# A hybrid encoder block: the first two token tiles normalised and transposed one by one, and the first loads in another order

## The chip, the cores and the metric

The kernel runs on one core of a Trainium2 chip. The metric is the device time of one execution in microseconds (us), lower is better; times shown are medians over runs. The engines are named as in the profile: PE is TensorE's matmul side and PEld its weight loads, DVE is VectorE, ACT is ScalarE, POOL is GpSimd, SP is SyncE, whose queue issues the loads of this part of the program.

## The reference, cut to what matters

One layer of a bidirectional encoder on 1024 tokens of width 1024, all in float32. Only its start is touched by the change: the first RMSNorm and the first columns of the combined input projection.

```python
def rmsnorm(x, g):
    xf = x.astype(jnp.float32)
    y = xf * lax.rsqrt(jnp.mean(xf * xf, axis=-1, keepdims=True) + EPS)
    return (y * g.astype(jnp.float32)).astype(x.dtype)
...
        h = rmsnorm(x, norm_mix[l])
        proj = h @ w_in[l]
        q, k, v, r, lr_f, lr_b, u, g_a, g_b = jnp.split(proj, split_points, axis=-1)
...
        o = (o * jax.nn.silu(r.astype(jnp.float32))).astype(x.dtype)
        y_a = o @ w_branch_gla[l]
...
        merged = jax.nn.sigmoid(g_a) * y_a + jax.nn.sigmoid(g_b) * y_b
        x = x + merged @ w_out[l]
        h2 = rmsnorm(x, norm_ffn[l])
        gate, up = jnp.split(h2 @ w_ffn_in[l], 2, axis=-1)
        x = x + (jax.nn.silu(gate) * up) @ w_ffn_out[l]
    return rmsnorm(x, norm_final)
```

Between the projection and `y_a` lies a gated linear attention in both directions with four heads, and beside it a pooling branch.

## The kernel before, in words

Every float32 product is made of three fp32r products: each operand is split into a high part (a cast on ACT) and a low part (the rest, a subtraction on DVE or POOL), and `mm3` (L293) issues high by high, high by low and low by high into one sum. Every instruction is written out by hand in the order in which its engine runs it; an engine works its list strictly in that order. Work that is to run beside matmuls stands in generators, which `pump` (L159), called after each `mm3`, advances by the columns that were multiplied; `begin` starts such a generator with a delay, `finish_side` runs the rest of it.

The 1024 tokens are eight tiles of 128, here called tile 0 to tile 7. Four buffers hold the raw tokens and four the normalised ones, so tile 4 uses the buffers of tile 0 (`x_126`, `xn_130` in the program's rows), tile 5 those of tile 1 (`x_127`, `xn_131`), 6 those of 2 (`x_128`, `xn_132`) and 7 those of 3 (`x_129`, `xn_133`). The first stage, which lasts to about 47 us, does this for every tile:

- **Norm** (`norm_x`, L393): ACT squares the tile with a row sum (L331), DVE adds the epsilon (`n1rs`, L322), POOL raises it to the power -0.5 (L323), DVE scales the tile (`xn`, L327). Then the load of the tile four further on is issued into the freed buffer. `norms` (L399) does two tiles as a generator.
- **Transposes** (`to_features`, L352, for a pair of tiles): for each of four pairs of feature blocks, four 128x128 transposes on PE (`transpose_tile`, L338) go into one PSUM bank, two for either tile. ACT then takes the bank out with the norm's gain as the high part `hh` (L345, two instructions of 128x256), DVE as the low part `hl` (L348, two of 128x256).
- **Values** (`first_values`, L415): eight feature blocks by three products, 24 matmuls of 288 columns (256 values of head 0 and 32 columns of the decay's low rank). The sum is split by ACT (`vh`, L198) and DVE (`vl`, L199), and ACT copies the low-rank columns (`lr`, L421); `lr` stands behind `vl` of the same tile.

The first weights come in four loads `raw` of 256 KB and one `lraw` of 128 KB with lines of 32 floats. Their high parts `fwh` are cast on ACT (L198, values) and POOL (L249, low rank), their low parts `fwl` made on DVE (the first two) and POOL (L199, L251).

Before the loop (L442 to L468) tiles 0 and 1 are normed and transposed together into four banks, and norms of 2 and 3 are written behind. In the loop over pairs (L469) the norms are two pairs ahead of their values: with tile 0 run the norms of 4 and 5, with tile 1 the transposes of 2 and 3, with tile 2 the norms of 6 and 7, with tile 3 the transposes of 4 and 5, with tile 5 those of 6 and 7. After tile 7 the projections of q and k of head 0 begin.

## Time and profile before

| what | value |
|---|---|
| median of 3 runs | 1399.84 us (1399.4 to 1400.83) |
| the profiled execution | 1400.29 us |
| its span, first to last instruction | 1398.6 us |
| PE busy | 1367.3 us, 98% of the span |
| PEld busy | 1152.5 us, 82% |
| DVE, ACT, POOL busy | 848.1, 624.0, 751.1 us |
| mean granted TensorE clock | 0.998 of full speed |

A row of the timeline gives the start, the time from start to end, engine, line, operation and operands of an instruction (or of a run of like ones, with xN), and in brackets how long the engine had been idle before it and what released it. Instructions of one engine overlap a little, so distances between starts say how fast it issues.

### The profile page before, as it was taken

How to read it: one execution, taken by the hardware profiler on the slowest of the kernel's cores; microseconds unless marked ns; L12 is line 12 of the kernel's file. 1: busy time of each engine (PE TensorE's matmuls, PEld its weight loads, DVE VectorE, ACT ScalarE, POOL GpSimd, SP SyncE). 2: the span in 40 equal slices, each digit the busy share in tenths (PEclk: the TensorE clock that was granted, in tenths of full speed). 3: DMA queues.
4: the chain of work that ended last, by engine and by line, in shares of the span. 5: the costliest groups of instructions: out<-in, count | busy, mean ns of one | idle time of the engine just before them, and what ended most of it. 6: DMA issues, size and time to landing. Idle time of an engine off the chain costs nothing. (4 is left out here: it accounts for less than half of the span.)

```text
span 1398.6 us, 18511 instructions
## 1 busy us (share of the span) xinstructions
PE 1367.3 (98%) x6654; PEld 1152.5 (82%) x6654; DVE 848.1 (61%) x1073; ACT 624.0 (45%) x1125; POOL 751.1 (54%) x565
## 2 busy tenths in 40 slices
PE   7999999999999999899999999999999999999997
PEld 6889898988888888788887888888888888888876
DVE  6266757667745885587875865556565556343364
ACT  6364655554334444455346633333333334453253
POOL 3261716041387555468665176666666667464364
PEclk9999999999999999999999999999999999999999
DMA  6211423322477668997425455554444447976461
GB/s 191 76 57 50 136 64 103 106 62 75 135 241 234 207 215 270 323 402 275 151 76 183 164 180 173 173 173 159 147 140 148 142 153 254 385 257 216 165 240 62
DMA packets 167453, 243.56 MB, mean 174 GB/s; under 512 B 10905, under 2 KB 97857, under 8 KB 167361
## 3 DMA queue, kind: packets, MB, share of 16 engines
q1 hardware_dynamic: 154944, 216.16, 46.3%
q10 hardware_dynamic: 12416, 26.22, 5.0%
q8 instruction: 52, 0.85, 0.3%
q14 instruction: 41, 0.33, 0.1%
HBM read 164.48 MB, written 77.86 MB: 173 GB/s over the span
## 5 line engine op out<-in xcount | busy, mean ns | idle before, releaser
L199 POOL TENSOR_TENSOR wl<-fs,wh 128x512 fp32r<-128x512 f32 x120 | 165.0, 1379 | 163.9 <-ACT wh L198 141.3
L291 PE MATMUL ps<-gl,wh 128*128 128x512 f32 x616 | 240.0, 390 | 0.8 <-DVE gl L1472 0.8
L291 PE MATMUL ps<-gh,wh 128*128 128x512 f32 x616 | 240.6, 391 | 0.0
L291 PE MATMUL ps<-gh,wl 128*128 128x512 f32 x616 | 239.9, 390 | 0.0
L199 POOL TENSOR_TENSOR wl<-fraw,wh 128x512 fp32r<-128x512 f32 x90 | 129.9, 1443 | 67.2 <-ACT wh L198 66.5
L199 POOL TENSOR_TENSOR ol<-gor,oh 128x1024 fp32r<-128x1024 f32 (+1 forms) x42 | 102.1, 2437 | 91.9 <-ACT oh L198 72.9
L291 PE MATMUL ps<-hh,wh 128*128 128x512 f32 x376 | 149.5, 398 | 0.0
L291 PE MATMUL ps<-hh,wl 128*128 128x512 f32 x376 | 146.8, 391 | 0.0
L291 PE MATMUL ps<-hl,wh 128*128 128x512 f32 x376 | 146.6, 390 | 0.0
L291 PEld LDWEIGHTS ps<-gl,wh 128*128 128x128 f32 x616 | 115.7, 188 | 24.9 <-DVE gl L1472 1.3
L291 PEld LDWEIGHTS ps<-gh,wl 128*128 128x128 f32 x616 | 115.7, 188 | 24.2
L199 POOL TENSOR_TENSOR wl<-raw,wh 128x512 fp32r<-128x512 f32 x44 | 61.4, 1411 | 137.7 <-ACT wh L198 135.2
L291 PEld LDWEIGHTS ps<-gh,wh 128*128 128x128 f32 x616 | 115.7, 188 | 23.6
L291 PE MATMUL ps<-oh,oh 128*128 128x512 f32 x308 | 120.0, 390 | 1.3 <-DVE x L1800 1.3
L291 PE MATMUL ps<-ol,oh 128*128 128x512 f32 x308 | 120.1, 390 | 0.2 <-DVE ol L199 0.2
L291 PE MATMUL ps<-oh,ol 128*128 128x512 f32 x308 | 119.9, 389 | 0.0
L199 POOL TENSOR_TENSOR wl<-wraw,wh 128x512 fp32r<-128x512 f32 x56 | 90.7, 1646 | 46.7 <-ACT wh L198 46.7
L199 DVE TENSOR_TENSOR ol<-wor,oh 128x1024 fp32r<-128x1024 f32 (+1 forms) x42 | 63.9, 1542 | 53.1 <-ACT oh L198 50.0
L198 ACT CAST wh<-fs 128x512 fp32r<-128x512 f32 x120 | 73.8, 615 | 30.8 <-DVE fs L902 23.1
L291 PEld LDWEIGHTS ps<-hh,wl 128*128 128x128 f32 x376 | 70.6, 188 | 15.1
L291 PEld LDWEIGHTS ps<-hl,wh 128*128 128x128 f32 x376 | 70.7, 188 | 13.4
L291 PEld LDWEIGHTS ps<-hh,wh 128*128 128x128 f32 x376 | 70.7, 188 | 13.4
(258 smaller groups left out, 3173.2 us busy)
## 6 DMA issues: line engine op xcount, KB each, us to landing
fraw<-in_w_ffn_in_dram SPq DMA_DIRECT2D x44, 512.0 KB, 6.4
gor<-g_out SPq DMA_DIRECT2D x35, 512.0 KB, 7.0
raw<-in_w_in_dram SPq DMA_DIRECT2D x48, 256.0 KB, 4.4
g_out<-s SPq DMA_DIRECT2D x44, 256.0 KB, 2.3
fraw<-in_w_in_dram SPq DMA_DIRECT2D x20, 512.0 KB, 4.2
wor<-t_out SPq DMA_DIRECT2D x20, 512.0 KB, 7.6
g_out<-g SPq DMA_DIRECT2D x33, 256.0 KB, 2.6
x<-in_x_dram SPq DMA_DIRECT2D x16, 512.0 KB, 3.9
```

What stands on the lines that cost most here:

```text
L198: nc.scalar.copy(hi, src)
L199: eng.tensor_tensor(lo, src, as_f32(hi), op=ALU.subtract)
L291: nc.tensor.matmul(ps, a[i], b[j], start=first and n == 0, stop=last and n == 2, skip_group_check=onto)
```

## The change

- **Loads.** The order on SP's queue is now tile 0, the norm's gain, the first two `raw`, `lraw`, the other two `raw`, and then tiles 1, 2 and 3. Tile 1 stood second before, and `lraw` behind all four `raw`.
- **Tiles 0 and 1 apart.** Each has its own two banks with four transposes each (`transpose_four`), and `hh` and `hl` of one feature block of one tile at a time, 128x128 (`gain_and_split_one`), eight of each per tile where eight of 128x256 served both. DVE's second low part of the weights stands between the second and third of these blocks of tile 0.
- **Squares apart from the norm.** `square_x` issues only ACT's part; `norm_x` does the rest.
- **Order of the rest.** Tile 1 is transposed behind the values of tile 0 on PE; the squares of 1, 2 and 3 stand behind tile 0's `hh` on ACT; DVE makes the norm of tile 3 between the fourth and fifth block of tile 1; the splits of the values of tile 0 stand behind all of this. The transposes of tiles 2 and 3 run beside the values of tile 1, from its fifth block on.
- **The loop** now starts at tile 2, and its norms are one pair ahead: those of 4 and 5 with tile 2, of 6 and 7 with tile 4. Their transposes run with tiles 3 and 5, as before.

From tile 2's first matmul on, PE's list is the same as before; ACT's differs up to the squares of 7, DVE's up to the norm of 7.

SP's queue at the start of the program; `x_126` to `x_129` are the loads of tiles 0 to 3. Before:

```order
L371 DMA x_126<-in_x_dram 128x1024
L374 DMA rows<-in_norm_mix_dram 8x128
L371 DMA x_127<-in_x_dram 128x1024
L206 DMA raw_141<-in_w_in_dram 128x2x256
L206 DMA raw_143<-in_w_in_dram 128x2x256
L206 DMA raw_145<-in_w_in_dram 128x2x256
L206 DMA raw_147<-in_w_in_dram 128x2x256
L384 DMA lraw_137<-in_w_in_dram 128x8x32
L371 DMA x_128<-in_x_dram 128x1024
L371 DMA x_129<-in_x_dram 128x1024
```

Now:

```order
L382 DMA x_126<-in_x_dram 128x1024
L388 DMA rows<-in_norm_mix_dram 8x128
L206 DMA raw_140<-in_w_in_dram 128x2x256
L206 DMA raw_142<-in_w_in_dram 128x2x256
L385 DMA lraw_137<-in_w_in_dram 128x8x32
L206 DMA raw_145<-in_w_in_dram 128x2x256
L206 DMA raw_147<-in_w_in_dram 128x2x256
L382 DMA x_127<-in_x_dram 128x1024
L382 DMA x_128<-in_x_dram 128x1024
L382 DMA x_129<-in_x_dram 128x1024
```

The load of tile 1 (`x_127`) moved from third place behind `lraw`, and `lraw` in front of the last two `raw`.

DVE behind the last `hl` of tile 0; `n1rs` and `xn` are the steps of a norm, `tr` a bank of transposes, `vl` the low part of a tile's values. Before (the `hl` of tiles 0 and 1 stand just ahead of this, all together):

```order
L322 TENSOR_SCALAR n1rs_254<-n1ms_252 128x1
L327 TENSOR_SCALAR xn_132<-x_128,n1rs_254 128x1024
L322 TENSOR_SCALAR n1rs_261<-n1ms_259 128x1
L327 TENSOR_SCALAR xn_133<-x_129,n1rs_261 128x1024
L322 TENSOR_SCALAR n1rs_275<-n1ms_273 128x1
L327 TENSOR_SCALAR xn_130<-x_126,n1rs_275 128x1024
L322 TENSOR_SCALAR n1rs_293<-n1ms_291 128x1
L327 TENSOR_SCALAR xn_131<-x_127,n1rs_293 128x1024
L199 TENSOR_TENSOR vl_162<-ps_266,vh_161 128x256
```

Now:

```order
L327 TENSOR_SCALAR n1rs_237<-n1ms_235 128x1
L332 TENSOR_SCALAR xn_131<-x_127,n1rs_237 128x1024
L327 TENSOR_SCALAR n1rs_269<-n1ms_242 128x1
L332 TENSOR_SCALAR xn_132<-x_128,n1rs_269 128x1024
L343 SCALAR_TENSOR_TENSOR hl_209<-tr_276,cols_173,hh_208 128x128 x2
L343 SCALAR_TENSOR_TENSOR hl_216<-tr_276,cols_173,hh_215 128x128 x2
L327 TENSOR_SCALAR n1rs_294<-n1ms_274 128x1
L332 TENSOR_SCALAR xn_133<-x_129,n1rs_294 128x1024
L343 SCALAR_TENSOR_TENSOR hl_222<-tr_277,cols_173,hh_221 128x128 x2
L343 SCALAR_TENSOR_TENSOR hl_228<-tr_277,cols_173,hh_227 128x128 x2
L199 TENSOR_TENSOR vl_162<-ps_244,vh_161 128x256
```

The norms of 4 and 5 (the third and fourth pair of rows before) are gone from here, those of 1 and 2 stand in their place, and the norm of 3 stands in the middle of tile 1's `hl`.

ACT from the squares of tiles 4 and 5 on (`xn_130,n1ms<-x_126` and `xn_131,n1ms<-x_127`); `vh` and `lr` are copies of a tile's finished values. Before, with the values of tiles 0 and 1 (`ps_266`, `ps_308`):

```order
L331 ACTIVATE xn_130,n1ms_273<-x_126 128x1024
L331 ACTIVATE xn_131,n1ms_291<-x_127 128x1024
L198 CAST vh_161<-ps_266 128x256
L421 COPY lr_158<-ps_266 128x128
L345 ACTIVATE hh_228<-tr_312,cols_173 128x256 x2
L345 ACTIVATE hh_234<-tr_327,cols_173 128x256 x2
L345 ACTIVATE hh_240<-tr_342,cols_173 128x256 x2
L345 ACTIVATE hh_246<-tr_357,cols_173 128x256 x2
L198 CAST vh_161<-ps_308 128x256
L421 COPY lr_158<-ps_308 128x128
L331 ACTIVATE xn_132,n1ms_389<-x_128 128x1024
L331 ACTIVATE xn_133,n1ms_407<-x_129 128x1024
```

Now, with the values of tiles 1, 2 and 3 (`ps_310`, `ps_386`, `ps_426`):

```order
L198 CAST vh_161<-ps_310 128x256
L446 COPY lr_158<-ps_310 128x128
L409 ACTIVATE xn_130,n1ms_390<-x_126 128x1024
L409 ACTIVATE xn_131,n1ms_408<-x_127 128x1024
L198 CAST vh_161<-ps_386 128x256
L446 COPY lr_158<-ps_386 128x128
L356 ACTIVATE hh_435<-tr_430,cols_173 128x256 x2
L356 ACTIVATE hh_452<-tr_447,cols_173 128x256 x2
L356 ACTIVATE hh_469<-tr_464,cols_173 128x256 x2
L356 ACTIVATE hh_486<-tr_481,cols_173 128x256 x2
L198 CAST vh_161<-ps_426 128x256
L446 COPY lr_158<-ps_426 128x128
```

The squares of 4 and 5 stood in front of `vh` of tile 0 and now stand behind `lr` of tile 1; those of 6 and 7 (`x_128`, `x_129`) moved from behind `lr` of tile 1 to behind `lr` of tile 3, just below the rows shown.

```diff
--- before.py
+++ after.py
@@ -198,7 +198,7 @@
         nc.scalar.copy(hi, src)
         eng.tensor_tensor(lo, src, as_f32(hi), op=ALU.subtract)
 
-    def load(src, kts, c0, width):
+    def load(src, kts, c0, width, and_then={}):
         per = min(HALF // width, kts)
         tiles = []
         for k0 in range(0, kts, per):
@@ -208,6 +208,7 @@
                 src[k0 * P : (k0 + per) * P, c0 : c0 + width].rearrange("(k p) c -> p k c", p=P),
             )
             tiles.append(raw)
+            and_then.get(len(tiles) - 1, bool)()
         return tiles
 
     class Weights:
@@ -241,8 +242,12 @@
             self.todo = tiles
             self.parts = [tuple(slot(F32R, (2, VL), s) for s in ("fwh", "fwl")) for _ in tiles]
 
-        def split_values(self, i, eng):
-            split_to(*(t[:, :, :DV] for t in self.parts[i]), self.todo[i][:, :, :], eng)
+        def high(self, i):
+            nc.scalar.copy(self.parts[i][0][:, :, :DV], self.todo[i][:, :, :])
+
+        def low_part(self, i, eng):
+            hi, lo = (t[:, :, :DV] for t in self.parts[i])
+            eng.tensor_tensor(lo, self.todo[i][:, :, :], as_f32(hi), op=ALU.subtract)
 
         def split_low(self):
             for i, (hi, _) in enumerate(self.parts):
@@ -326,10 +331,16 @@
     def scale_by(dst, src, rs):
         nc.vector.tensor_scalar(dst[:, :], src, rs[:, :], None, op0=ALU.mult)
 
-    def norm_scale(xt, sq, s):
-        ms = vec(1, s + "ms")
-        nc.scalar.activation(sq[:, :], xt, AF.Square, scale=1.0 / 32.0, accum_out=ms[:, :])
-        return rms_scale(ms[:, :], 1, s + "rs")
+    def transpose_four(ps, xt, k0):
+        for k in range(4):
+            nc.tensor.transpose(ps[:, k * P : (k + 1) * P], xt[:, (k0 + k) * P : (k0 + k + 1) * P], ident[:, :])
+
+    def gain_and_split_one(ps, k, t, act, gain):
+        c = slice((t % 4) * P, (t % 4 + 1) * P)
+        hi, lo = act(k, t // 4)
+        src, g = ps[:, (k % 4) * P : (k % 4 + 1) * P], gain[:, k : k + 1]
+        nc.scalar.activation(hi[:, c], src, AF.Copy, scale=g)
+        nc.vector.scalar_tensor_tensor(lo[:, c], src, g, as_f32(hi[:, c]), op0=ALU.mult, op1=ALU.subtract)
 
     def transpose_tile(ps, xt, i, kp):
         for kk in range(2):
@@ -349,14 +360,14 @@
                 lo[:, c], src, g, as_f32(hi[:, c]), op0=ALU.mult, op1=ALU.subtract
             )
 
-    def to_features(xn, t0, act, gain):
+    def to_features(xn, t0, act, gain, every=1):
 
         for kp in range(KT // 2):
             ps = bank(ps_g, "tr")
             for i in range(2):
                 transpose_tile(ps, xn[i], i, kp)
             gain_and_split(ps, kp, t0, act, gain)
-            yield 1
+            yield every
 
 
     xt = [slot(shape=(D,), s="x") for _ in range(4)]
@@ -370,6 +381,9 @@
     def load_x(t):
         nc.sync.dma_start(xt[t % 4][:, :], x[t * P : (t + 1) * P, :])
 
+    def load_low():
+        nc.sync.dma_start(lraw[:, :, :], w_in[:, LR0:U0].rearrange("(k p) c -> p k c", p=P))
+
     def load_rows(tile, at, v, n):
         nc.sync.dma_start(tile[at : at + n, :], v[0].rearrange("(j p) -> j p", p=P))
 
@@ -379,10 +393,8 @@
 
     load_x(0)
     load_rows(rows[0], 0, norm_mix, 8)
-    load_x(1)
-    first_raw = load(*next(order))
-    nc.sync.dma_start(lraw[:, :, :], w_in[:, LR0:U0].rearrange("(k p) c -> p k c", p=P))
-    for t in (2, 3):
+    first_raw = load(*next(order), and_then={1: load_low})
+    for t in (1, 2, 3):
         load_x(t)
     for i, (v, n) in enumerate(vec_rows):
         load_rows(rows[1], sum(n for _, n in vec_rows[:i]), v, n)
@@ -390,8 +402,18 @@
 
     hT = Activations("h")
 
+    sums_of = {}
+
+    def square_x(t):
+        sums_of[t] = vec(1, "n1ms")
+        nc.scalar.activation(
+            xn[t % 4][:, :], xt[t % 4][:, :], AF.Square, scale=1.0 / 32.0, accum_out=sums_of[t][:, :]
+        )
+
     def norm_x(t):
-        rs = norm_scale(xt[t % 4][:, :], xn[t % 4], "n1")
+        if t not in sums_of:
+            square_x(t)
+        rs = rms_scale(sums_of.pop(t)[:, :], 1, "n1rs")
         scale_by(xn[t % 4], xt[t % 4][:, :], rs)
         if t + 4 < NT:
             load_x(t + 4)
@@ -417,6 +439,9 @@
         ps = bank(ps_mm)
         for kt in range(KT):
             mm3(ps[:, :VL], tokens(hT(kt, t // 4), t), w(kt), kt == 0, kt == KT - 1)
+        return ps
+
+    def split_values(v, t, ps):
         split_to(*(part[:, t % 4, :] for part in v[t // 4]), ps[:, :DV])
         nc.scalar.copy(low_rows[:, t, :, :], ps[:, DV:VL].unsqueeze(1).broadcast_to([P, 4, 2 * RANK]))
 
@@ -453,34 +478,49 @@
     g_mix = cols[0]
     g_ffn, g_gla, g_pool = (cols[1][:, 8 * i : 8 * i + 8] for i in range(3))
     b_dec = (cols[1][:, 24:28], cols[1][:, 28:32])
-    norm_x(1)
-    trs = [bank(ps_g, "tr") for _ in range(KT // 2)]
-    for t in range(2):
-        for kp, ps in enumerate(trs):
-            transpose_tile(ps, xn[t], t, kp)
     w = FirstWeights(first_raw, lraw)
     w.split_low()
     for i in range(KT // 2):
-        w.split_values(i, nc.vector if i < 2 else nc.gpsimd)
-    for kp, ps in enumerate(trs):
-        gain_and_split(ps, kp, 0, hT, g_mix)
+        w.high(i)
+    w.low_part(0, nc.vector)
+
+    def features_of(t, between={}):
+
+        trs = [bank(ps_g, "tr") for _ in range(2)]
+        for i, ps in enumerate(trs):
+            transpose_four(ps, xn[t], 4 * i)
+        for k in range(KT):
+            gain_and_split_one(trs[k // 4], k, t, hT, g_mix)
+            between.get(k, bool)()
+
+    features_of(0, {1: partial(w.low_part, 1, nc.vector)})
+    for i in (2, 3):
+        w.low_part(i, nc.gpsimd)
+    norm_x(1)
+    square_x(2)
+    ps = first_values(w, v, 0)
     norm_x(2)
-    norm_x(3)
-    for t in range(0, NT, 2):
-        if t + 4 < NT:
-            begin(norms(t + 4), 1)
+    square_x(3)
+    features_of(1, {3: partial(norm_x, 3)})
+    split_values(v, 0, ps)
+    begin(to_features(xn[2:], 2, hT, g_mix, 0.6), 1.8)
+    ps = first_values(w, v, 1)
+    finish_side()
+    split_values(v, 1, ps)
+    vectors(1, 8)
+    for t in range(2, NT, 2):
+        if t + 2 < NT:
+            begin(norms(t + 2), 0.5)
         if t == 2:
             for d, w_up in enumerate((w_decay_up_fwd, w_decay_up_bwd)):
                 for i in range(3):
                     load_up(i, d, w_up)
             fetch()
-        first_values(w, v, t)
+        split_values(v, t, first_values(w, v, t))
         finish_side()
-        if t == 0:
-            vectors(1, 8)
         if t + 2 < NT:
             begin(to_features(xn[(t + 2) % 4 :], t + 2, hT, g_mix), 0.5)
-        first_values(w, v, t + 1)
+        split_values(v, t + 1, first_values(w, v, t + 1))
         finish_side()
         if t == 4:
             up_weights()
```

## The prediction

> **What bounds the kernel now.** I read the timeline of the first 50 us engine by engine, then the waits of PE. PE is busy for 98% of the span, so nearly every microsecond that its list starts or stalls later moves the end by as much; what counts is when PE reaches the first row behind which it runs as before. I take as that mark the fourth group of transposes beside tile 5, at 39.88 us, since no engine that PE waits for behind it has its list changed.
>
> The head first. On ACT the last weights end a wait for a load, then `hh` of tiles 0 and 1 follows:
>
> ```profile
> 10.53 0.62 ACT L198 CAST fwh<-raw 128x512 fp32r<-128x512 f32 x1 [0.28 <-DMA raw<-in_w_in_dram]
> 11.06 3.02 ACT L345 ACTIVATE hh<-tr,cols 128x256 fp32r<-128x256 f32 x8
> 13.92 1.10 ACT L331 ACTIVATE xn<-x 128x1024 f32<-128x1024 f32 x1
> ```
>
> PE's first value matmul and the place where its spacing halves:
>
> ```profile
> 11.80 0.59 PE L291 MATMUL ps<-fwh,hh 128*128 128x288 f32 x1
> ...
> 13.76 0.44 PE L291 MATMUL ps<-fwh,hh 128*128 128x288 f32 x1
> 14.00 0.34 PE L291 MATMUL ps<-fwl,hh 128*128 128x288 f32 x1
> ```
>
> So the fourth `raw` sets the start: its cast at 10.53, `hh` 0.53 later, the first matmul at 11.80. Matmuls then come every 0.24 us until about 14.0. Then, at tile 3's norm on DVE and its transposes on PE, PE waits:
>
> ```profile
> 17.71 0.75 DVE L327 TENSOR_SCALAR xn<-x,n1rs 128x1024 f32<-128x1024 f32 x1 [0.67 <-POOL n1rs L323]
> ```
>
> ```profile
> 18.52 0.44 PE L338 MATMUL tr<-ident,xn 128*128 128x128 f32 x2 [0.87 <-DVE n1rs L322]
> 18.71 0.38 PE L291 MATMUL ps<-fwh,hh 128*128 128x288 f32 x1
> ```
>
> From `xn` to the transposes it is 0.81, to the next matmul 0.19 more. How long two norms in a row take is seen where nothing else disturbs them, at tiles 6 and 7; first ACT, where the squares start 0.16 behind the start of `lr`, then DVE:
>
> ```profile
> 26.42 0.27 ACT L421 COPY lr<-ps 128x128 f32<-128x128 f32 x1 [1.18 <-DVE vl L199]
> 26.58 1.06 ACT L331 ACTIVATE xn<-x 128x1024 f32<-128x1024 f32 x1
> ```
>
> ```profile
> 27.76 0.15 DVE L322 TENSOR_SCALAR n1rs<-n1ms 128x1 f32<-128x1 f32 x1 [1.38 <-ACT xn L331]
> 28.58 0.75 DVE L327 TENSOR_SCALAR xn<-x,n1rs 128x1024 f32<-128x1024 f32 x1 [0.66 <-POOL n1rs L323]
> 29.25 0.14 DVE L322 TENSOR_SCALAR n1rs<-n1ms 128x1 f32<-128x1 f32 x1
> 30.05 0.75 DVE L327 TENSOR_SCALAR xn<-x,n1rs 128x1024 f32<-128x1024 f32 x1 [0.66 <-POOL n1rs L323]
> ```
>
> From the first square to the second tile's transposes: 1.18 + 0.82 + 0.67 + 0.80 + 0.81 = **4.28 us**, and 0.19 more to PE's next matmul: 4.47. Before, this lies beside values of other tiles: these norms are transposed only with tile 5, beginning at 36.17.
>
> Last, the end of a pair (tile 5) on PE, ACT and DVE:
>
> ```profile
> 36.17 0.60 PE L338 MATMUL tr<-ident,xn 128*128 128x128 f32 x4
> 36.53 0.38 PE L291 MATMUL ps<-fwh,hh 128*128 128x288 f32 x1
> ...
> 39.88 0.60 PE L338 MATMUL tr<-ident,xn 128*128 128x128 f32 x4
> ...
> 40.71 0.29 PE L291 MATMUL ps<-fwh,hh 128*128 128x288 f32 x1
> ...
> 43.91 0.30 PE L291 MATMUL ps<-fwh,hh 128*128 128x288 f32 x1
> ```
>
> ```profile
> 40.52 0.84 ACT L345 ACTIVATE hh<-tr,cols 128x256 fp32r<-128x256 f32 x2 [0.41 <-PE tr L338]
> 41.25 0.37 ACT L198 CAST vh<-ps 128x256 fp32r<-128x256 f32 x1
> 42.63 0.27 ACT L421 COPY lr<-ps 128x128 f32<-128x128 f32 x1 [1.02 <-DVE vl L199]
> ```
>
> ```profile
> 41.39 0.88 DVE L348 SCALAR_TENSOR_TENSOR hl<-tr,cols,hh 128x256 fp32r<-128x256 f32 x2 [0.38 <-ACT hh L345]
> 42.18 0.42 DVE L199 TENSOR_TENSOR vl<-ps,vh 128x256 fp32r<-128x256 f32 x1
> ```
>
> Call the start of the fourth group G (39.88). The next tile begins at G + 0.83 and its 24 matmuls take 3.20 (40.71 to 43.91, 0.133 each). Meanwhile `hh`, `hl`, `vl`, `lr` of the finished tile follow one another, and `lr` starts at G + 2.75. From the first group's matmul to the fourth group it is 39.88 - 36.53 = 3.35.
>
> **The change, part by part.**
>
> *Loads.* Bytes moved from the start to three moments:
>
> ```profile
> 0.00:8.20 8.20, 1.15 (x5) 1.09 (x6) 3.78 (x9) 3.27 (x4) 3.64 (x38) 1.00 0.71 237
> 0.00:9.30 9.30, 2.21 (x9) 1.75 (x9) 3.93 (x10) 4.37 (x7) 4.16 (x39) 1.00 0.79 245
> 0.00:10.50 10.50, 2.53 (x11) 2.07 (x12) 5.06 (x12) 5.23 (x8) 4.19 (x39) 1.00 0.81 253
> ```
>
> The last number is GB/s: 1.94, 2.28 and 2.66 MB. Up to the fourth `raw` the queue held 2 tiles and 4 `raw`, 2 x 0.52 + 4 x 0.26 = 2.10 MB, so 0.56 MB of later loads had moved by then too. Now it holds one tile, four `raw` and `lraw`, 1.70 MB. With the same surplus it is there at 2.26 MB, **9.3 us**; with a surplus of 0.24 at 8.2; if sharing takes the whole gain, at 10.5 as now. I take 9.3, since the surplus is measured. The loads of tiles 4 to 7 and all behind them on SP are issued about as before; their users come more than 5 us later. The rate while `lraw` was being issued:
>
> ```profile
> 4.05 1.04 SPq L384 DMA_DIRECT2D lraw<-in_w_in_dram  x1
> ```
>
> ```profile
> 4.00:5.00 1.00, 0.24 (x1) 0.18 (x1) 0.71 (x4) 0.59 (x1) 0.00 (x0) 1.00 1.02 352
> 5.00:6.00 1.00, 0.00 (x0) 0.00 (x0) 0.15 (x1) 0.56 (x2) 0.10 (x1) 1.00 0.88 291
> ```
>
> It dips by 17%, which the surplus above holds already. [...]
>
> *Tile 0.* ACT casts the last `raw` at 9.3, `hh` starts at 9.8, and the first matmul at about 10.3: **1.5 us sooner** than 11.80. Eight `hh` of 128x128 are new: each between 0.16 (the step behind the 128x128 `lr`) and 0.36 (11.06 to 13.92, eight of 128x256); I take 0.25, near the middle, together 2.0. PE needs to 14.0 for 15 matmuls at 0.24 and 1.2 more for nine at 0.133: tile 0 ends at 15.2.
>
> *Tile 1.* Its chain, not PE, sets the pace now. Squares of 1, 2 and 3 on ACT at 11.8, 12.85, 13.9 (1.10 each, overlapping a little). DVE: `n1rs` of 1 at 11.8 + 1.18 = 12.98, `xn` 13.80, `n1rs` of 2 14.47, `xn` 15.28, free at 15.95. PE transposes tile 1 from 15.2, the first bank is full at 15.65, `hh` out of it at 16.0. Four `hl` of 128x128 at 0.28 (between half and all of 0.395, which is (42.18 - 41.39) / 2) end at 17.15, and only then `n1rs` of tile 3 comes, 0.82 later its `xn`: **X = 18.0**. POOL's parts of the weights, which stand ahead of the norms' power, I take as done by 13.2. PE, whose fifth block of tile 1 stands behind tile 3's transposes, waits for X + 0.81.
>
> *Behind X.* DVE goes on at X + 0.67 with four `hl` (1.12), `vl` of tile 0 at X + 1.79, ACT's `lr` 0.45 later at 2.24, `hh` of tiles 2 and 3 at 2.40, their `hl` 0.87 later at 3.27, eight of them 3.16, `vl` of tile 1 at 6.43, `lr` 6.88, and 0.16 later the square of tile 4: X + 7.04. Before, this square lay under tile 0's values. Its chain lets PE go on at X + 7.04 + 4.47 = X + 11.51. PE alone would be there at X + 1.0 + four blocks of 0.40 + three groups of 0.44 + 0.25 for the vectors + 3.20 + 0.40 + 0.36 = X + 8.1: a **new stall of 3.4 us** in tile 3. The fourth group is at X + 11.51 + 3.35 = X + 14.86.
>
> *Tiles 4 and 5.* The same again without the late start: squares of 6 at G + 2.75 + 0.16 = G + 2.91, PE goes on at G + 7.38; alone it would at G + 0.83 + 3.20 + 0.40 + 0.36 = G + 4.79. A **second stall, 2.6 us**. The next fourth group is at G + 10.73. What queues behind the late norms on DVE, `vl` of the tile and `hl` of the next pair, comes before PE needs it.
>
> *Sum.* X + 14.86 + 10.73 = 18.0 + 25.6 = 43.6 instead of 39.88: **+3.7 us**. What goes with it is counted in this: the old waits behind tile 1 and before tile 4 are gone. The profiled execution took 1400.29, so 1404.0; the median is 0.45 lower, so **1403.5**. Bounds: the load alone moves X by -1.1 to +1.2, `hh` by -0.7 (0.16) to +0.9 (0.36). With the larger of the two at its end, 1402.4 to 1404.7; that is this case's own range. About 0.2%, 2.8 us, is what a measurement of this kernel can tell from no change: under 1397.0 or over 1402.6.
>
> **The rivals.**
>
> *The head's gain survives.* If squares, norms and splits follow each other 2.6 to 3.4 us faster than the rows say, the two stalls vanish, and 1403.5 - 6.0 = 1397.5 remains. It decides whether the second norm is ready by G + 4.4, where PE wants it, or at G + 7.2. For it speaks only that the norms of 4 and 5 depend on no load; against it every step of the chain, since all are measured one behind the other.
>
> *The weights come no sooner.* The loads share the engines, and the fourth `raw` stays at 10.5: X is 19.2, and 1404.7 results.
>
> *The clock drops in the stalls.* After one long wait the matmuls of 512 columns restart at 0.43 instead of 0.23:
>
> ```profile
> 577.82 0.79 PE L291 MATMUL ps<-trh,wh 128*128 128x512 f32 x1 [3.77 <-ACT ga L1265]
> 578.41 0.63 PE L291 MATMUL ps<-trl,wh 128*128 128x512 f32 x1
> 578.84 0.63 PE L291 MATMUL ps<-trh,wl 128*128 128x512 f32 x1
> ```
>
> If 2.6 us in two pieces do what 3.77 did, half rate for the 2.2 us seen at the start (11.80 to 14.00) costs 1.1 to 1.2 twice, 1405.8. The 0.87 at 18.52 did nothing. [...]
>
> *The delay is taken up later.* Then half of it or all goes, 1401.7 to 1399.8. Against it: of PE's waits for a DMA behind 48 us there is this one,
>
> ```profile
> PE yb L291 <- DMA pl<-p_out: 0.3, 1, 0.3
> ```
>
> and the rest are for engines that PE feeds.
>
> **How the numbers follow.** Chances: forecast 0.56, head survives 0.14, weights no sooner 0.13, clock 0.05, taken up 0.12. Three quarters of the forecast's own range lie over 1402.6 (0.42), with the weights and the clock 0.60 slower; the rest of it 0.14, the delay taken up 0.12 and 0.09 of the head's case are 0.35 the same; the head's case with an early fourth `raw` (1397.5 - 1.1) gives 0.05 faster. The range runs from 1400.5, inside the case of a delay taken up, to 1406.0, over the clock's price; it leaves out the head's case and a small part beside.
>
> **What the profile of the changed kernel would show.** First value matmul near 10.3; `xn` of tile 3 near 18.0; PE idle before the transposes of tiles 4 and 5 (after three matmuls of tile 3) for some 3 us in two pieces, released by DVE, and the same at tiles 6 and 7 for 2.6; the fourth group of tile 5 near 43.6; equal distances behind it. Wrong if the squares of tile 4 start before `lr` of tile 1, if these transposes wait less than a microsecond, or if the fourth group is before 40.

## The result and the profile after

The change made the kernel slower by about 13.6 us: 1413.9 us (median of 4, 1411.21 to 1416.2) against 1400.34 of the kernel before, a ratio of 1.0094 with a 95% interval of 1.0081 to 1.0106. The sign was forecast, the size was not: 1403.5 was predicted, and 1406.0 was the upper end. The profiled execution took 1413.42 us with a span of 1411.7, 13.1 more than before. The mark of the prediction, the fourth group of transposes beside tile 5, went from 39.88 to 53.33, 13.45 later. So the loss arises ahead of the mark, and hardly any of it (0.35) is given back behind it.

The head of the changed kernel, on ACT: `hh` of tile 0, one 128x128 block at a time, and the first square behind it. The bracket is the idle time before the instruction and what ended it.

```profile
9.32 0.36 ACT L342 ACTIVATE hh<-tr,cols 128x128 fp32r<-128x128 f32 x1
10.10 0.37 ACT L342 ACTIVATE hh<-tr,cols 128x128 fp32r<-128x128 f32 x1 [0.42 <-DVE hl L343]
10.89 0.37 ACT L342 ACTIVATE hh<-tr,cols 128x128 fp32r<-128x128 f32 x1 [0.42 <-DVE hl L343]
12.69 0.62 ACT L342 ACTIVATE hh<-tr,cols 128x128 fp32r<-128x128 f32 x2 [1.44 <-DVE hl L343]
13.74 0.37 ACT L342 ACTIVATE hh<-tr,cols 128x128 fp32r<-128x128 f32 x1 [0.42 <-DVE hl L343]
14.52 0.37 ACT L342 ACTIVATE hh<-tr,cols 128x128 fp32r<-128x128 f32 x1 [0.42 <-DVE hl L343]
15.31 0.37 ACT L342 ACTIVATE hh<-tr,cols 128x128 fp32r<-128x128 f32 x1 [0.42 <-DVE hl L343]
15.57 1.05 ACT L409 ACTIVATE xn<-x 128x1024 f32<-128x1024 f32 x1
```

The eight blocks take 6.25 us (9.32 to 15.57) and not 2.0: an `hh` comes every 0.786 us, and in six of eight places ACT stands idle for DVE's `hl` of the block before. The fourth and the fifth block come together (`x2` at 12.69): the fifth is the first of the second PSUM bank (PE writes its results into PSUM; the kernel puts four of these blocks into one bank of it), and it waits for no `hl`. The longest gap, 1.44, has its reason on DVE, whose second low part of the weights stands between two `hl` and takes 1.62. The last row is `xn` of tile 3:

```profile
10.50 0.35 DVE L343 SCALAR_TENSOR_TENSOR hl<-tr,cols,hh 128x128 fp32r<-128x128 f32 x1 [0.43 <-ACT hh L342]
10.77 1.62 DVE L250 TENSOR_TENSOR fwl<-raw,fwh 128x512 fp32r<-128x512 f32 x1
12.32 0.34 DVE L343 SCALAR_TENSOR_TENSOR hl<-tr,cols,hh 128x128 fp32r<-128x128 f32 x1
...
23.36 0.75 DVE L332 TENSOR_SCALAR xn<-x,n1rs 128x1024 f32<-128x1024 f32 x1 [0.66 <-POOL n1rs L328]
```

X, the start of `xn` of tile 3, is 23.36 where 18.0 was predicted. Behind it, on PE, come the stalls at the transposes of tiles 4 and 5 and of 6 and 7:

```profile
34.78 0.41 PE L349 MATMUL tr<-ident,xn 128*128 128x128 f32 x2 [2.54 <-DVE n1rs L327]
36.17 0.69 PE L349 MATMUL tr<-ident,xn 128*128 128x128 f32 x2 [0.98 <-DVE xn L332]
36.51 0.59 PE L296 MATMUL ps<-fwh,hh 128*128 128x288 f32 x1
36.90 0.44 PE L296 MATMUL ps<-fwl,hh 128*128 128x288 f32 x1
37.14 0.44 PE L296 MATMUL ps<-fwh,hl 128*128 128x288 f32 x1
...
42.51 0.60 PE L349 MATMUL tr<-ident,xn 128*128 128x128 f32 x4
...
48.23 0.44 PE L349 MATMUL tr<-ident,xn 128*128 128x128 f32 x2 [1.14 <-DVE n1rs L327]
49.78 0.44 PE L349 MATMUL tr<-ident,xn 128*128 128x128 f32 x2 [1.10 <-DVE xn L332]
...
53.33 0.60 PE L349 MATMUL tr<-ident,xn 128*128 128x128 f32 x4
```

Both stalls are where they were forecast, in two pieces and released by DVE. What is new is behind the first: matmuls of 288 columns start 0.24 apart (36.90 to 37.14) where the kernel before has 0.133 (40.71 to 43.91 for 24), and the way from the first group's matmul to the fourth group is 6.0 us (36.51 to 42.51) where before needed 3.35. The windows say why; their third number from the end is the granted clock:

```profile
26.00:36.00 10.00, 6.35 (x43) 5.23 (x41) 5.94 (x16) 6.67 (x18) 1.10 (x2) 0.97 0.56 166
36.00:48.00 12.00, 10.93 (x62) 10.66 (x62) 5.01 (x13) 6.50 (x16) 0.55 (x1) 0.74 0.00 1
```

### The profile page after: what moved, and what is told of

The parts are those of the page before. It is cut to its first block, busy times and chain, and to the rows that moved or that the text cites. A ratio compares the mean times of both kernels' runs of the same rounds, so it can differ in the third digit from the quotient of the medians.

```text
span 1411.7 us, 18521 instructions
## 1 busy us (share of the span) xinstructions
PE 1374.7 (97%) x6654; PEld 1159.6 (82%) x6654; DVE 844.8 (60%) x1081; ACT 627.2 (44%) x1133; POOL 751.5 (53%) x565
## 4 chain that ended last, share of the span: by engine, by line
PE 68%; DVE 4%; DMA 2%; POOL 2%; issue 2%; ACT 2%; ACTq 0%; SPq 0%; POOLq 0%; DVEq 0%
PE ps L296 66%; DMA wor<-t_out 1%; DMA u_out<-uph 1%; POOL wl L199 1%; PE tp L1032 0%; DMA ph<-p_out 0%; PE op L873 0%; DVE x L1596 0%; PE yb L296 0%; POOL n3rs L1579 0%; POOL mg L1223 0%; ACT wh L198 0%; POOL gl L1512 0%; DVE upl L658 0%; ACT hb L1530 0%
```

## The experiments

The theory for the head: ACT and DVE take turns on one bank, since in the program's list of instructions every `hh` waits for the `hl` before it in the same bank. Its rivals: the wait hangs on something other than the bank, such as the buffer of `hh` that two blocks share; or the new loads are to blame. For the rest, the late norms and the clock behind them. The list of the changed kernel on ACT, with its waits (`tr_198` and `tr_199` are the two banks of tile 0; the first instruction's wait for DVE is for the gain in `cols`):

```
L342 ACTIVATE hh_208<-tr_198,cols_173 128x128 [waits DVE_49,PE_49]
L342 ACTIVATE hh_208<-tr_198,cols_173 128x128 [waits DVE_49]
L342 ACTIVATE hh_215<-tr_198,cols_173 128x128 [waits DVE_49] x2
L342 ACTIVATE hh_221<-tr_199,cols_173 128x128 [waits PE_49]
L342 ACTIVATE hh_221<-tr_199,cols_173 128x128 [waits DVE_49]
L342 ACTIVATE hh_227<-tr_199,cols_173 128x128 [waits DVE_49] x2
```

Every `hh` waits for DVE, but for the fifth, the first of its bank. These are waits that are written into the program, each for a semaphore that DVE raises. In the kernel before no `hh` behind the first has such a wait.

**All four `hh` of a bank, then its four `hl`** (`e1_bank_then_low`): the new last argument of `gain_and_split_one` says which half it issues, `False` for `hh` and `True` for `hl`.

```diff
-        for k in range(KT):
-            gain_and_split_one(trs[k // 4], k, t, hT, g_mix)
-            between.get(k, bool)()
+        for b, ps in enumerate(trs):
+            for k in range(4 * b, 4 * b + 4):
+                gain_and_split_one(ps, k, t, hT, g_mix, False)
+            for k in range(4 * b, 4 * b + 4):
+                gain_and_split_one(ps, k, t, hT, g_mix, True)
+                between.get(k, bool)()
```

> Edit: per bank the four high parts first, then the four low parts; nothing else. Theory (same-bank wait): in the changed kernel each hh of a bank waits for DVE's hl of the block before it, 0.79 us a block instead of 0.25. Without the wait the eight hh of tile 0 take about 2 us, xn of tile 3 starts near 18 instead of 23.4, the fourth group of tile 5 comes at 43.6 to 46.3 instead of 53.3 (the upper end if the clock still drops in tile 3), and the time is 7 to 10 us under the changed kernel, 1404 to 1407. Rival (late norms alone): the alternation costs nothing, since tile 1 waits for its squares anyway, and all of the loss is the late norms of tiles 4 to 7 and the clock; then the time stays at 1412 to 1414.

Measured: 1407.37 us (1405.86 to 1411.39), ratio 1.0046 (1.0029 to 1.0063). ACT:

```profile
9.14 2.17 ACT L343 ACTIVATE hh<-tr,cols 128x128 fp32r<-128x128 f32 x8
11.16 1.10 ACT L411 ACTIVATE xn<-x 128x1024 f32<-128x1024 f32 x1
...
18.13 2.18 ACT L343 ACTIVATE hh<-tr,cols 128x128 fp32r<-128x128 f32 x8 [3.71 <-PE tr L336]
```

Eight `hh` in 2.02 us (9.14 to 11.16), 0.25 each as in the prediction's sum, and half of the loss is gone; the time is just above the 1404 to 1407 that were expected. The profiled execution is the slowest of the four (1411.39), and its places are those of a slow one. In it X came at 21.16 and not at 18.0. DVE now begins a bank's `hl` only behind its four `hh`, the second low part of the weights behind two of them starts at 10.84 (at 9.72 with the four banks below), and PE waits for both; tile 0 ran at half rate from end to end (0.24 between its matmuls but for PE's waits, 10.02 to 16.80), and its 24 matmuls held the transposes of tile 1 up to 17.04 (ACT's wait of 3.71). So this order cures the wait and, in this execution, pays elsewhere.

**Alternation kept, four banks a tile, so that neighbours never share one** (`e2_four_banks`): blocks k and k + 4 share a bank.

```diff
-        src, g = ps[:, (k % 4) * P : (k % 4 + 1) * P], gain[:, k : k + 1]
+        src, g = ps[:, (k // 4) * P : (k // 4 + 1) * P], gain[:, k : k + 1]
...
-        trs = [bank(ps_g, "tr") for _ in range(2)]
-        for i, ps in enumerate(trs):
-            transpose_four(ps, xn[t], 4 * i)
+        trs = [bank(ps_g, "tr") for _ in range(4)]
+        for k in range(KT):
+            c = slice(k // 4 * P, (k // 4 + 1) * P)
+            nc.tensor.transpose(trs[k % 4][:, c], xn[t][:, k * P : (k + 1) * P], ident[:, :])
         for k in range(KT):
-            gain_and_split_one(trs[k // 4], k, t, hT, g_mix)
+            gain_and_split_one(trs[k % 4], k, t, hT, g_mix)
```

> Edit: hh and hl alternate as in the changed kernel, but a tile has four banks, blocks k and k+4 in one. Theory (same-bank wait): neighbours in the order share no bank, so ACT doesn't wait; like the first experiment within 1 us, 1404 to 1408. Second form of the theory (the wait is for the hh tile, which blocks 0 and 1, 2 and 3 and so on share): every second block waits still, half of the gain, 1408 to 1411. Rival (late norms alone): 1412 to 1414.

Measured: 1405.05 us (1403.33 to 1407.69), ratio 1.0034 (1.0021 to 1.0047). ACT, then `xn` of tile 3 on DVE:

```profile
8.80 1.66 ACT L342 ACTIVATE hh<-tr,cols 128x128 fp32r<-128x128 f32 x6
11.44 0.63 ACT L342 ACTIVATE hh<-tr,cols 128x128 fp32r<-128x128 f32 x2 [0.99 <-DVE hl L343]
...
15.58 2.18 ACT L342 ACTIVATE hh<-tr,cols 128x128 fp32r<-128x128 f32 x8 [0.40 <-PE tr L492]
...
24.90 1.06 ACT L409 ACTIVATE xn<-x 128x1024 f32<-128x1024 f32 x1
```

```profile
17.96 0.75 DVE L332 TENSOR_SCALAR xn<-x,n1rs 128x1024 f32<-128x1024 f32 x1 [0.67 <-POOL n1rs L328]
```

The instructions of ACT and DVE, their order and their buffers of `hh` are those of the change; only the bank differs, and 8.9 us of the 13.6 are gone. The wait is one for the bank, and it is the largest part of the loss. The one wait that is left, 0.99, is the seventh `hh`'s, whose bank holds the third block, and that block's `hl` stands behind the weights' low part. X is at 17.96 (predicted 18.0), the square of tile 4 at X + 6.94 (predicted X + 7.04). Part of that fit is luck: the first matmul came at 9.30 and not at 10.3, and ACT's 0.99 behind the weights' low part used that up. The fourth group of tile 5 came 1.5 later than predicted, for which the clock runs below give the reason:

```profile
45.09 0.60 PE L349 MATMUL tr<-ident,xn 128*128 128x128 f32 x4
```

**The loads in the old order, the rest as changed** (`e3_old_loads`):

```diff
-    first_raw = load(*next(order), and_then={1: load_low})
-    for t in (1, 2, 3):
+    load_x(1)
+    first_raw = load(*next(order))
+    load_low()
+    for t in (2, 3):
         load_x(t)
```

> Edit: the changed kernel with the loads in the order of before (tile 1 third, lraw behind all raw). Theory: the new load order is worth what it moves, the last raw lands some 2 us later and with it the first value matmul (9.8 to about 11.8): 1415 to 1417. Rival (the new load order itself costs time, since tile 1 and what is behind it lands late): 1410 to 1413.

Measured: 1412.21 us (1410.99 to 1413.79), ratio 1.0085 (1.007 to 1.01), not to be told apart from the change. The first value matmul comes 1.85 later (11.68 against 9.83), but X only 0.67 later (24.03). The later start that was expected is there, but not the 1415 to 1417. One reason is in the trace: here DVE's second low part takes 0.68 and not 1.62, while POOL's two of the same size come later (from 13.69), and the eight `hh` take 5.31 and not 6.25. With the bank wait in force, the loads do not matter much.

**PE kept busy in the first stall** (`e4_busy_gap`): twelve matmuls of 512 columns whose sum nobody reads, ahead of the transposes of tiles 4 and 5 (`keep_hot`, filled further down, holds two slices of tile 0's `hh`).

```diff
...
     def to_features(xn, t0, act, gain, every=1):
+        if t0 == 4:
+            for _ in range(12):
+                nc.tensor.matmul(vps[:, :], keep_hot[0], keep_hot[1], start=True, stop=True)
```

> Edit: the changed kernel with twelve matmuls of 512 columns into an unused part of a bank just ahead of the transposes of tiles 4 and 5, where PE waits for the norms; their result is read by nobody. Theory (the half rate from 36.5 to 42.2 comes from PE idling in front of it): PE works through the gap, the half rate is gone, 2 to 3 us less than the changed kernel, about 1411. Rival (the half rate has another cause, or PE had no time for them): no gain, or up to 2.7 us more, 1413 to 1417.

Measured: 1414.39 us (1411.61 to 1415.73), ratio 1.0097 (1.0082 to 1.0112): nothing won. The windows from 26 to 36 and from 44 to 52 us, the granted clock third from the end:

```profile
26.00:36.00 10.00, 8.95 (x55) 7.46 (x53) 5.90 (x16) 6.70 (x18) 1.10 (x2) 1.00 0.57 167
...
44.00:52.00 8.00, 5.73 (x32) 5.25 (x32) 3.69 (x9) 3.40 (x10) 1.10 (x2) 0.79 0.01 3
```

The half rate behind the first stall is gone: tile 3's fourth group comes at 39.79 and not at 42.51. In this execution it appears behind the second, where the change had none, and from there to the mark it is 12.40 and not 10.82. On the time the run is inconclusive; it made me ask whether a stall drops the clock each time or only in some places.

**Late norms alone, in the kernel before** (`e5_late_norms_only`):

```diff
-        if t + 4 < NT:
-            begin(norms(t + 4), 1)
+        if t and t + 2 < NT:
+            begin(norms(t + 2), 0.5)
```

> Before, with one thing changed: the norms of tiles 4 and 5 and of 6 and 7 begin as late as in the change (with the tile ahead of their transposes). Loads and head are those of before. Theory (a late norm stalls PE, and nothing takes the stall up later): the squares of tile 4 follow `lr` at 26.42, the transposes of tile 5 come at 30.9 where PE is there at 26.8, so a stall of 3.5 us in two pieces, another of 1.5 to 2.5 at tiles 6 and 7, fourth group beside tile 5 at 45 to 46.5, and 1.5 more for each stall behind which the clock drops: 1405.5 to 1408.5. Rival (the delay is taken up later): within 1 us of before, 1399.4 to 1401.4. Rival (the late norms cost little in themselves, and the loss is in the head): the stalls are under 1 us and the time is under 1402.

Measured: 1404.27 us (1402.72 to 1406.24), ratio 1.0031 (1.002 to 1.0043). PE, at the transposes of tiles 4 and 5 and of 6 and 7:

```profile
26.50 0.44 PE L338 MATMUL tr<-ident,xn 128*128 128x128 f32 x2 [1.14 <-DVE n1rs L322]
27.98 0.69 PE L338 MATMUL tr<-ident,xn 128*128 128x128 f32 x2 [1.04 <-DVE xn L327]
...
38.79 0.44 PE L338 MATMUL tr<-ident,xn 128*128 128x128 f32 x2 [1.14 <-DVE n1rs L322]
40.27 0.44 PE L338 MATMUL tr<-ident,xn 128*128 128x128 f32 x2 [1.04 <-DVE xn L327]
...
43.82 0.60 PE L338 MATMUL tr<-ident,xn 128*128 128x128 f32 x4
```

The waits stand at the same two places as in the change, with the old head, the old loads and no bank wait: 4.36 us in four pieces. The second stall is nearly that of the change (1.14 + 1.04 against 1.14 + 1.10), the first is shorter (1.14 + 1.04 against 2.54 + 0.98). The mark is 3.9 later than before and the time 3.7. Shown: the late norms cost by themselves, and neither is their delay taken up later nor is it a loss of the head. The time is under my 1405.5; in the profiled execution (1402.96) the head was 1.0 sooner (first matmul at 10.77) and the first stall was 2.2 and not 3.5, which would account for it.

**Four banks and early norms** (`e6_early_norms`): on ACT the squares of 4 and 5 stand between `vh` and `lr` of tile 0, where ACT idled for `vl`, those of 6 and 7 between `vh` and `lr` of tile 2; the rest of each norm follows as early on DVE.

```diff
-    def split_values(v, t, ps):
+    def split_values(v, t, ps, early=()):
         split_to(*(part[:, t % 4, :] for part in v[t // 4]), ps[:, :DV])
+        for e in early:
+            square_x(e)
+        for e in early:
+            scale_of[e] = rms_scale(sums_of.pop(e)[:, :], 1, "n1rs")
...
-    split_values(v, 0, ps)
+    split_values(v, 0, ps, (4, 5))
...
+    scale_by(xn[0], xt[0][:, :], scale_of[4])
     split_values(v, 1, ps)
+    scale_by(xn[1], xt[1][:, :], scale_of[5])
...
-        if t + 2 < NT:
-            begin(norms(t + 2), 0.5)
```

> The four-bank form of the change, and in it the squares of tiles 4 and 5 stand on ACT between `vh` and `lr` of tile 0, those of 6 and 7 between `vh` and `lr` of tile 2, with the rest of each norm as early on DVE; all else as there. Theory (bank wait, late norms and the clock behind them are the whole loss, and the earlier head is a true gain): `xn` of tile 3 stays near 18.0, no stall over 0.5 us at the transposes of tiles 4 to 7, no half clock behind 13 us, fourth group beside tile 5 near 37.5, so 2.4 us sooner than before: 1397.5 to 1399. Rival (a delay or a gain in the head is taken up later): 1400 to 1401 although the fourth group is sooner. Rival (ACT's squares ahead of `lr` hold up `hh` of the next pair, and the stall only moves there): fourth group at 40 or later, 1400.5 to 1403.

Measured: 1398.9 us (median of 10, 1397.28 to 1400.18) against 1400.57 of before, ratio 0.9988 (0.9978 to 0.9997): 6.2 us under the four banks alone, and faster than before. PE no longer waits there:

```profile
26.91 0.60 PE L349 MATMUL tr<-ident,xn 128*128 128x128 f32 x4
...
38.77 0.60 PE L349 MATMUL tr<-ident,xn 128*128 128x128 f32 x4
```

X was 18.47, so the fourth group at 38.77 is X + 20.3, where the change's sum had X + 25.6. Of the 2.4 us forecast over before, 1.1 arrived at the mark, and the medians differ by 1.7; tile 0's half rate (0.24 between its matmuls and not 0.13) lasted to 15.0 here (to 12.1 in the four-bank run), which may be where a part of the rest went. So the change's 13.6 come apart into 8.9 for the bank wait and 6.2 for the late norms with the clock behind them, less about 1.5 that the new head gains.

**PE kept busy in both stalls, four banks** (`e7_hot_stalls`): as in the earlier run of this kind, ten matmuls, and the condition `t0 > 2`.

> The four-bank form of the change, with ten matmuls 128x512 whose result nobody uses ahead of the first transposes of tiles 4 and 5 and of 6 and 7, so that PE is busy in both stalls. Theory (half clock behind a stall is a loss of its own, 1.5 us in the four-bank run): no half-rate matmuls between 20 and 45 us, fourth group beside tile 5 at 43.6 as predicted, 1403.0 to 1404.0. Rival (the clock behind the stalls is no loss at the end, or only moves to a later place): 1405, as without them.

**Four banks, old loads** (`e8_four_banks_old_loads`): the edit on the loads shown above, made on the four banks.

> The four-bank form of the change with the loads in the order of before (tile 0, tile 1, weights, low-rank weights, tiles 2 and 3). Theory (with the bank wait gone the arrival of the weights sets the head): first value matmul near 11.1 instead of 9.30, `xn` of tile 3 near 19.5 instead of 17.96, fourth group beside tile 5 1.5 later, 1406 to 1407. Rival (the load order is worth nothing even then, since tile 1 comes sooner and the half clock ends at the same time): 1404.5 to 1405.5, and `xn` of tile 3 within 0.5 of 17.96.

Measured: with busy stalls 1404.54 us (1401.93 to 1405.94), ratio 1.0029 (1.0017 to 1.0042); with old loads 1406.16 us (1403.18 to 1411.2), ratio 1.0039 (1.0026 to 1.0051). By the times alone neither is told apart from the four banks (1.0034); with busy stalls the time missed the 1403 to 1404 of the theory. The profiles do more, though each shows one execution, for the busy stalls the slowest of six (1405.94), for the old loads one of the fastest of ten (1403.88). The windows from 26 to 36 us of the four banks, of the busy stalls and of the old loads:

```profile
26.00:36.00 10.00, 7.77 (x49) 7.31 (x48) 4.91 (x12) 5.24 (x14) 1.10 (x2) 0.83 0.35 99
```

```profile
26.00:36.00 10.00, 9.87 (x70) 9.17 (x69) 5.89 (x14) 5.66 (x17) 1.10 (x2) 1.00 0.35 100
```

```profile
26.00:36.00 10.00, 7.76 (x60) 7.32 (x59) 5.60 (x16) 5.83 (x15) 1.10 (x2) 1.00 0.42 115
```

And PE's waits in the four banks; then, for the busy stalls, X on DVE and the fourth group on PE; then the same of the old loads, with its waits:

```profile
27.80 0.41 PE L349 MATMUL tr<-ident,xn 128*128 128x128 f32 x2 [1.26 <-DVE n1rs L327]
29.19 0.69 PE L349 MATMUL tr<-ident,xn 128*128 128x128 f32 x2 [0.98 <-DVE xn L332]
```

```profile
18.26 0.75 DVE L332 TENSOR_SCALAR xn<-x,n1rs 128x1024 f32<-128x1024 f32 x1 [0.66 <-POOL n1rs L328]
```

```profile
43.85 0.60 PE L349 MATMUL tr<-ident,xn 128*128 128x128 f32 x4
```

```profile
20.91 0.75 DVE L332 TENSOR_SCALAR xn<-x,n1rs 128x1024 f32<-128x1024 f32 x1 [0.66 <-POOL n1rs L328]
```

```profile
30.76 0.41 PE L349 MATMUL tr<-ident,xn 128*128 128x128 f32 x2 [1.26 <-DVE n1rs L327]
32.15 0.44 PE L349 MATMUL tr<-ident,xn 128*128 128x128 f32 x2 [0.98 <-DVE xn L332]
...
46.52 0.60 PE L349 MATMUL tr<-ident,xn 128*128 128x128 f32 x4
```

The two kernels have the same waits to 0.01 us, 1.26 and 0.98. In one execution the clock fell behind them, in the other it did not. From X to the fourth group it is 45.09 - 17.96 = 27.13 with the drop, 46.52 - 20.91 = 25.61 without it, and 43.85 - 18.26 = 25.59 where PE was kept busy; the prediction's sum was 25.6. So this drop cost 1.5 us, and a stall of this length may or may not bring one. From 26 to 58 us of the twelve profiles of this case the clock fell (matmuls of 288 columns 0.24 apart and not 0.13) behind eight of fourteen stalls of 1.6 to 3.5 us, and nowhere else. With the old loads X is at 20.91, later than the 19.5 expected and 2.95 later than in the new order; the medians differ by 1.1.

**The bank wait kept, norms early** (`e9_bank_wait_early_norms`): the edit of the early norms, made on the change itself.

> The change as it is, with the wait between `hl` and `hh` of a bank, and in it only the early norms of the run before (squares of 4 and 5 between `vh` and `lr` of tile 0, of 6 and 7 between `vh` and `lr` of tile 2). Theory (the two losses are apart and add up): `xn` of tile 3 stays near 23.4 as in the change, behind it 20.3 to the fourth group beside tile 5 as in the early-norms run, so 43.7 there, 3.8 later than before: 1403.5 to 1406 by where the clock falls. Rival (with the head so late the norms are hidden or exposed differently, so the stalls stay): fourth group at 48 or later, 1408 or more.

Measured: 1407.28 us (1406.07 to 1409.2), ratio 1.0047 (1.0033 to 1.0061). In time the two losses add up (6.6 us by early norms here, 6.2 with four banks), but the time is over the 1403.5 to 1406 of my theory, and so is the mark: X at 23.36, as expected, the fourth group at 46.95 and not at 43.7. ACT, then PE:

```profile
26.50 1.07 ACT L409 ACTIVATE xn<-x 128x1024 f32<-128x1024 f32 x1
...
28.73 3.05 ACT L356 ACTIVATE hh<-tr,cols 128x256 fp32r<-128x256 f32 x8
```

```profile
29.27 0.40 PE L296 MATMUL ps<-fwh,hh 128*128 128x288 f32 x1 [1.26 <-ACT hh L356]
```

With `hh` of tile 1 stretched by the bank wait, ACT has no idle time left for the two squares; they hold `hh` of tiles 2 and 3 up to 28.73, PE waits 1.26 for it, and in this execution the clock dropped behind it (0.83 of full speed on average from 26 to 36 us). What is free in one form has a price in the other.

**Early norms, old loads** (`e10_early_norms_old_loads`): the edit on the loads, made on the fastest form.

> The fastest form so far (four banks, early norms) with the loads in the order of before. Theory (in this form the arrival of the weights sets the head, 1.0 to 1.9 us as seen in the first value matmul of the runs with one and with the other order): `xn` of tile 3 at 19.5 to 20.9 instead of 18.47, fourth group beside tile 5 at 40 to 41, 1400 to 1401.5. Rival (the load order is worth nothing): 1398.4 to 1399.4.

Measured: 1401.85 us (median of 11, 1398.5 to 1402.71), ratio 1.0002 (0.9993 to 1.0011), against 0.9988 in the new order. X came at 20.37 and not at 18.47, the fourth group at 40.67 and not at 38.77. So once the bank wait and the stalls are gone, the new load order is worth 1.9 us at the mark and about as much in the time, and without it the form is no faster than before.

## Why the prediction was wrong

By its steps, in the profiled execution:

| step | predicted | measured |
|---|---|---|
| first value matmul | 10.3 | 9.83 |
| eight `hh` of tile 0 | 2.0 (0.25 each) | 6.25 |
| squares of 1, 2, 3 start | 11.8, 12.85, 13.9 | 15.57, 16.61, 17.65 |
| X, `xn` of tile 3 | 18.0 | 23.36 |
| square of tile 4 | X + 7.04 | X + 8.53 (31.89) |
| PE goes on in tile 3 | X + 11.51 | X + 13.15 (36.51) |
| first group to fourth group, tile 3 | 3.35 | 6.0 |
| from there to the fourth group of tile 5 | 10.73 | 10.82 |
| that group | 43.6 | 53.33 |

**The step that failed: "Eight `hh` of 128x128 are new ... I take 0.25".** The duration was right, 0.25 where they follow each other (2.02 and 2.18 for eight in the runs above). What I left out is that the change lets `hh` and `hl` take turns, block by block, on a bank that four blocks share, and that in the program's list ACT's next read of a bank waits for DVE's read before it. The pace became 0.786. That is six times 0.53 = 3.2, and 1.0 more because DVE's second low part stands in this ring and took 1.62 (with 0.68, in the run with the old loads, the eight took 5.31): 4.2 us in tile 0, against 0.5 that the start was sooner. In tile 1 the same ring cost 1.5 ahead of X (from its first `hh` to X 3.83 us, 19.53 to 23.36, against 2.38 with four banks) and, in the last four blocks behind X, 1.6 more (the square of tile 4 at X + 8.53 against X + 6.94). The kernel with four banks shows the sum: without it X is back at 17.96, and the time falls by 8.9 us, to 1405.05, which the forecast's 1400.5 to 1406.0 would have held.

At the mark the sum was 9.73 short (53.33 for 43.6). Of that X is 5.36, the square of tile 4 behind it 1.49, the half rate behind the first stall 2.65, and all the rest 0.23. So the clock is a second term that the sum put at nothing.

The trace of before had the sign of it, and I quoted it: `lr` at 42.63 stands idle 1.02 for DVE's `vl`, and both only read the sum `ps`. I used that as a fact about `lr` and did not ask why one read should wait for another. Before, no such wait fell on `hh`, since both `hh` of a bank stood ahead of both its `hl`. In the trace of the change ACT stands idle 0.42 us or more before every `hh` but a bank's first; where neighbours have separate banks, one such wait is left in sixteen (0.99). The waits are the program's, and no run lets these reads alternate on one bank without them, so what the chip would do then is not shown.

**The late norms: right.** Two stalls were forecast at 3.4 and 2.6 us; the waits were 2.54 + 0.98 and 1.14 + 1.10, and the way from tile 3's fourth group to tile 5's was 10.82 for 10.73. The late norms alone, in the old kernel, stall PE at the same two places (2.2 us each) and cost 3.7 us, and early norms take 6.2 us off.

**The clock: a rival given 0.05 that came true once.** I bounded it by one wait of 3.77, behind which matmuls of 512 columns came at 0.43 and not at 0.23. That these shorter stalls would most likely cost nothing beyond the waits themselves was my estimate, and the runs do not bear it out: behind waits of 1.26 and 0.98 the clock dropped in one execution and not in another, and behind 2.54 and 0.98 it did here (0.74 in the windows, 2.65 us on the way to the fourth group). The price I named, 1.1 to 1.2 a stall, was too small: 1.5 in the four-bank run, 2.65 in the change.

**The weights come sooner: right.** The first value matmul stands at 9.30 to 10.26 in the seven profiles with the new order (mean 9.84) and at 10.55 to 11.80 in the five with the old (mean 11.25), 1.4 sooner where 1.5 was forecast. But with the bank wait in force the earlier start shows no effect in the time (1.0085 against 1.0094).

**The other rivals.** That the delay is taken up later fell: the mark moved by 13.45 and the span by 13.1. That the head's gain survives fell for this change; the early-norms run shows how much of it there was to have, 1.7 us at the end. The direction, slower, came out for the reason forecast as far as the late norms go; most of the loss has the other reason.

## What to carry to other kernels

When a change alternates two engines on the same data, look at which PSUM bank each reads: the program may make a read wait for another engine's read of that bank, and the pace is then the sum of both durations and the handovers (here 0.37 + 0.35 and 0.07 in all). Read what an instruction waits for in the changed list, not only how long it takes in the old trace; and of a wait in the old trace ask why it is there before using its number. A step moved out of the way is free only where its engine idles: the same two squares cost nothing in one form and 1.26 us of PE in the other.

## What the runs showed of the hardware that I had not expected

- **Two reads of one bank by ACT and DVE in turn, each waiting for the other by a semaphore:** 0.786 us a block of 128x128 (0.37 and 0.35 and the handovers), against 0.25 where neighbouring blocks lie in separate banks.
- **The same stall drops the clock in one execution and not in another.** The same two waits of 1.26 and 0.98 gave a mean clock of 0.83 from 26 to 36 us in one execution and 1.00 in another. What tells the two apart is not shown. Later stages have such places too: two windows of the run with busy stalls and the same two of the run with four banks and old loads, the clock third from the end:

```profile
230.00:250.00 20.00, 18.03 (x124) 16.89 (x123) 12.34 (x23) 11.13 (x26) 12.81 (x11) 0.91 0.15 52
575.00:600.00 25.00, 20.83 (x82) 16.60 (x81) 13.27 (x17) 12.10 (x22) 9.29 (x8) 0.86 0.98 343
```

```profile
230.00:250.00 20.00, 17.80 (x128) 16.10 (x127) 14.05 (x26) 10.55 (x22) 11.92 (x12) 1.00 0.17 53
575.00:600.00 25.00, 22.17 (x97) 17.95 (x96) 15.34 (x20) 13.22 (x23) 11.82 (x9) 1.00 0.96 343
```

  From the mark to the end of the span it is 1404.2 - 43.85 = 1360.35 in the first and 1402.2 - 46.52 = 1355.7 in the second. The clock in the two windows can account for that (as an estimate, with PE busy all the time, 0.09 x 20 + 0.14 x 25 = 5.3), but no run changes it alone. So some 4 us of a single execution may hang on this, and differences of 1 to 2 us between kernels need the mark in the trace beside the median.
- **A low part of 128x512 on DVE took 0.68 to 0.70 us ahead of POOL's two of this size and 1.62 beside them.** In the change DVE's first, from 7.12, took 0.70, and the second, from 10.77, 1.62, with POOL in its two from 9.35 to 11.85; with the old loads DVE's took 0.69 and 0.68 (from 8.88 and 12.59), and POOL's two began at 13.69. With the four banks DVE's second took 1.42 (from 9.72), and with a bank's four `hh` first 1.83 (from 10.84); POOL was busy in both from 8 to 12 without a gap (4.00 of 4.00). In the change this lay in the ring of `hh` and `hl`. That the two hinder each other is only seen, not tested.
